# Seven-product MLP: where operand sums, stored parts, gate loads and down-step preparations stand in the program order

## The chip, the cores and the metric

The kernel runs on one core of a Trainium2 chip. The metric is the device time of one execution in microseconds (us); lower is better. A core has five engines that each work through their own list of instructions in order and wait for one another on semaphores: TensorE (PE, matrix products), VectorE (DVE), ScalarE (ACT), GpSimd (POOL) and SyncE (SP, which here only starts transfers). ACT and POOL can start transfers too; each of the three has a queue of its own, and the profile counts 16 DMA engines that carry them.

## The reference

Two transformer layers on 1024 tokens of width 1024. What bears on the change is the end of the first layer:

```
m  = g0 * y_a + g1 * y_b + g2 * y_c         # y_b = attn @ w_b
h  = h + m @ w_o
hn = rms_norm(h, norm2_g)
gate, up = split(hn @ w_gate_up)            # w_gate_up 1024 x 5632
h  = h + (silu(gate) * up) @ w_down         # w_down 2816 x 1024
mkv = rms_norm(mem) @ w_mem_kv              # second layer, prepared early
```

## The kernel before

Every float32 product is made of three passes: each operand is split into a high part (a rounded copy, made by ACT) and a low part (what is left, a subtraction, made by POOL or DVE, `lo_of`, L312). `mm3` (L283, L284, L285) issues high x high, high x low (or low x high) and low x high. A weight goes from a loaded tile `wraw` into two parts `wpart`: ACT L96 and POOL L97 for the plain stages, ACT L1233 and POOL L312 for the gate/up products.

The stages follow each other on PE in program order: **wb** (attention output times `w_b`), **mkv** (the memory projection, in two halves), **wo** (output projection, added to `h`), **mlp** (gate/up), **down**, and then the second layer. What each engine does is written out by hand, one call after the other; pools hand out the buffers, and an engine that is given an instruction whose input or buffer isn't ready waits, with all that stands behind it.

*wb.* 16 tiles of 128 x 512. Each needs a stored gate (`g1d`) and a stored partial sum (`mpart`), loaded one tile ahead by `load_gp` into two of four `ev` buffers. DVE L1079 multiplies the product with the gate, L1080 adds the partial sum, ACT L1081 makes the high part, POOL L312 the low part. Beside it run two side jobs that are advanced as PE work is issued: one that normalizes the memory rows `mrow` (ACT L316, DVE L1039) for PE to transpose (L1045), and one that builds a bias table `G` and writes it out (ACT L1027, `gd<-G`, 768 KB out of 4 partitions).

*wo.* Per token block t (8 of them, 128 tokens) and quarter j of the columns, `add_rows` adds the product to `h` (DVE L1140). `norm2_a` takes the sum of squares of both halves of a block's row (ACT L316) and stores it, `norm2_b` finishes the RMS norm (DVE, up to L329).

*mlp.* Gate/up and down are block products of 2 x 2 blocks made with seven products instead of eight (Winograd's form). The blocks of `hn` are (first or last four token blocks) x (first or second half of the columns). Each of the seven products p takes a sum of blocks as its moving operand, turned on PE (`turns`, L1146, into two `ax` buffers) and split by ACT L1149 and DVE L1150 into `tb` or `tm`. `T1` (POOL L1179) and `T3` (DVE L1180) are two of these sums, `sums24` (DVE L1497, POOL L1498) makes two more. The sums of the weights' blocks are `gu_sums` (DVE L1208 to L1210). One product (`gu_mm(n)`) is 12 matmuls of 512 columns; `gu_seq` is the order of the 154 products: unit 0 (gate) and unit 1 (up) of the first 256 columns are interleaved, all later units come one after the other. `gu_prep(n)` splits the weights of product n, `gu_out(n)` evacuates it. After each up unit, `hidden_sums` (POOL L1338 to L1341) makes the hidden blocks and sums that the down stage needs, and `store` writes them to DRAM (`hd`): three of the seven (`SPLIT`) as a high part (ACT L1303) and a low part (DVE L312). `at(n, f)` puts a store off to product n.

*down.* 77 steps (7 products x 11 pairs), four token blocks each, 12 matmuls of 512 columns a step. `dn_ahead(m)` loads step m+8, sums the weights of m+4 (L1450), makes high parts of m+3 (ACT L1466) and low parts of m+2 (DVE L312). `dn_open` does that for the first steps, ahead of the last two `gu_out`. The final norm of the first four blocks runs beside the last steps (DVE L329).

Of the kernel before, what the change touches and what calls it, by code (L numbers as in the profile page):

```python
# [117 lines left out]
def build(tc, A, out, dbg=None, stop=None):  # L118
# [1042 lines left out]
    ssq = {}  # L1161

    def norm2_a(t):

        ssq[t] = [work.tile([128, 4], F32, name="ss", bufs=4)[:, :1] for _ in range(2)]
        for c in range(2):
            sumsq(ht[t, c], ssq[t][c])
            nc.sync.dma_start(hres[t, :, 512 * c:512 * c + 512], ht[t, c])

    def norm2_b(t):  # L1170

        s0, s1 = ssq.pop(t)
        nc.vector.tensor_tensor(s0, s0, s1, op=ALU.add)
# [16 lines left out]
    gu_seq = [(0, 1), (0, 2), (1, 1), (1, 2)] + [(u, p) for p in (5, 7, 3, 4, 6) for u in (0, 1)]  # L1190
# [47 lines left out]
    for j in range(4):  # L1238
# [44 lines left out]
    acc, todo = {}, []  # L1283
# [14 lines left out]
    def store(p, pr, t):  # L1298
        if p not in SPLIT:
            nc.sync.dma_start(hd[p - 1, pr, :, :512], t)  # L1300
# [3 lines left out]
        lo_of(t.bitcast(F32R), t, hi, nc.vector)  # L1304
        nc.sync.dma_start(hd[p - 1, pr, :, :512], hi.bitcast(F32))
# [25 lines left out]
    def hidden_sums(u, n):  # L1331
# [84 lines left out]
    def dn_load(m):  # L1416
# [3 lines left out]
        p, i = dn_seq[m]  # L1420
        f1, f2 = (slice((2 * i + c) * 128, (2 * i + c) * 128 + 128) for c in (0, 1))
# [72 lines left out]
    def sums24(ts):

        for t in ts:
            nc.vector.tensor_tensor(ht[t + 4, 1], ht[t + 4, 1], ht[t, 0], op=ALU.subtract)  # L1497
            nc.gpsimd.tensor_tensor(ht[t, 1], ht[t, 1], ht[t + 4, 1], op=ALU.subtract)  # L1498
# [9 lines left out]
    gu_prep(5)  # L1508
    gu_mm(2, [(7, 0), (7, 1), (7, 2), (5, 3)])
    gu_out(2)  # L1510
    gu_mm(3, [(3, 3), (7, 3), (6, 0), (6, 1)])
    sums24((3,))
# [12 lines left out]
    for n in range(6, last - 1):
# [11 lines left out]
    run_todo(last + 9)  # L1537
    close(hbp)
    close(tbp)
# [3 lines left out]
    hpool = pool("h2", side="right")  # L1543
    h = hpool.tile([128, NT, D], F32, name="hh")
# [4 lines left out]
    hxp = pool("hx", side="right")  # L1549
    fg = hxp.tile([128, D], F32, name="fg")  # L1550
# [494 lines left out]
```

## Time and profile before

| what | value |
|---|---|
| time, median of 3 runs | 2262.42 us (2260.66 to 2262.77) |
| the profiled execution's own time | 2258.33 us |
| its span in the trace | 2256.6 us |
| busy: PE, DVE, POOL, ACT | 96%, 61%, 37%, 35% |
| mean granted TensorE clock | 0.986 of full |

The span is the time between the first and the last instruction that the trace shows; 1.73 us lie around it. Busy shares are means over the whole span. A matmul of 512 columns shows a duration of about 0.4 us, but the next one starts 0.23 us after it, since they are pipelined: distances between starts tell the pace. "PEclk" is the share of full speed that the clock throttle granted.

### The profile page before, as it was taken

Reading aid. Unit: us, or ns where it says so; the run is one execution under the profiler, and the core shown is the slowest. Engines: PE = TensorE matmul, PEld = TensorE weight load, DVE = VectorE, ACT = ScalarE, POOL = GpSimd, SP = SyncE. Lnnn points to the kernel's source line nnn. Section 1 sums busy time; section 2 is a strip of 40 time slices with the busy share of each in tenths; the row PEclk is TensorE's granted clock in tenths of the full one; section 3 lists DMA queues with packets and bytes.
Section 4 is the critical chain, followed back from the end, with each engine's and each line's share of the span. In section 5 each row is a group of like instructions: output and inputs, shape, how many; then the busy total and the mean of one; then the engine's idle time right before and its main releaser. Section 6 shows DMA issues by size and latency. Waiting matters only on the chain.

```text
span 2256.6 us, 31373 instructions
## 1 busy us (share of the span) xinstructions
PE 2166.0 (96%) x11855; PEld 1872.9 (83%) x11855; DVE 1382.1 (61%) x2712; ACT 785.9 (35%) x1548; POOL 840.0 (37%) x713
## 2 busy tenths in 40 slices
PE   7999999999999999989779999999999999999998
PEld 6789888998888888779767888888788799997998
DVE  6688899888883887321754545454675650922724
ACT  4573211211122876221232333333433342212631
POOL 0213322325542310852146878777100212661122
PEclk9999999999999999999889999999999999999999
DMA  4212122113320000444212433333998612120023
GB/s 146 70 66 73 57 77 76 48 47 103 109 88 19 20 1 10 161 120 158 80 42 84 145 108 128 125 112 106 322 341 320 207 57 80 38 66 19 1 70 137
DMA packets 150076, 227.84 MB, mean 101 GB/s; under 512 B 14896, under 2 KB 93972, under 8 KB 149924
## 3 DMA queue, kind: packets, MB, share of 16 engines
q1 hardware_dynamic: 131872, 179.85, 24.0%
q0 software_dynamic: 8096, 26.74, 3.2%
q10 hardware_dynamic: 9956, 19.24, 2.5%
q8 instruction: 93, 1.52, 0.3%
q14 instruction: 59, 0.48, 0.1%
HBM read 170.46 MB, written 55.31 MB: 100 GB/s over the span
## 4 chain that ended last, share of the span: by engine, by line
PE 84%; issue 4%; DVE 4%; DMA 3%; POOL 3%; ACT 2%; ACTq 0%; DVEq 0%; SPq 0%; POOLq 0%
PE mm L285 24%; PE mm L284 24%; PE mm L283 24%; PE ax L283 2%; PE ax L285 2%; PE ax L284 2%; PE mm L956 1%; PE ax L1928 1%; DMA ev<-mpart 1%; PE mm L1870 1%; POOL wpart L97 1%; PE mm L337 1%; DMA ev<-g1d 1%; DVE scores L565 1%; PE mm L1906 1%
## 5 line engine op out<-in xcount | busy, mean ns | idle before, releaser
L97 POOL TENSOR_TENSOR wpart<-wraw,wpart 128x1024 fp32r<-128x1024 f32 (+1 forms) x108 | 259.4, 2420 | 531.1 <-ACT wpart L96 510.9
L285 PE MATMUL mm<-xh,wpart 128*128 128x512 f32 (+2 forms) x736 | 269.9, 367 | 0.0
L284 PE MATMUL mm<-xl,wpart 128*128 128x512 f32 (+2 forms) x736 | 269.5, 366 | 0.0
L283 PE MATMUL mm<-xh,wpart 128*128 128x512 f32 (+2 forms) x736 | 269.0, 365 | 0.0
L608 DVE MAX8 m<-scores 128x8 f32<-128x272 f32 (+6 forms) x224 | 188.8, 843 | 6.4 <-POOL scores L570 0.2
L610 DVE MATCH_REPLACE8 scores<-m,scores 128x272 f32<-128x272 f32 (+6 forms) x224 | 185.0, 826 | 0.0
L283 PE MATMUL mm<-tm,wpart 128*128 128x512 f32 x440 | 175.2, 398 | 5.4 <-DVE ev L1392 5.4
L285 PE MATMUL mm<-tm,wpart 128*128 128x512 f32 x440 | 174.4, 396 | 0.0
L284 PE MATMUL mm<-tm,wpart 128*128 128x512 f32 x440 | 174.3, 396 | 0.0
L96 ACT ACTIVATE wpart<-wraw 128x1024 fp32r<-128x1024 f32 (+1 forms) x110 | 111.5, 1048 | 150.7 <-issue 80.5
L284 PEld LDWEIGHTS mm<-xl,wpart 128*128 128x128 f32 x736 | 138.5, 188 | 20.5
L283 PEld LDWEIGHTS mm<-xh,wpart 128*128 128x128 f32 x736 | 138.3, 188 | 20.3
L285 PEld LDWEIGHTS mm<-xh,wpart 128*128 128x128 f32 x736 | 138.3, 188 | 19.5
L283 PE MATMUL mm<-wpart,hh 128*128 128x256 f32 x512 | 142.6, 278 | 0.0
L284 PE MATMUL mm<-wpart,hh 128*128 128x256 f32 x512 | 142.2, 278 | 0.0
L285 PE MATMUL mm<-wpart,hl 128*128 128x256 f32 x512 | 142.1, 278 | 0.0
L312 POOL TENSOR_TENSOR wpart<-hb,wpart 128x512 fp32r<-128x512 f32 x88 | 119.0, 1360 | 36.0 <-ACT wpart L1233 36.0
L284 PE MATMUL mm<-wpart,tm 128*128 128x512 f32 x242 | 97.1, 401 | 9.8 <-DVE wpart L312 9.8
L283 PEld LDWEIGHTS mm<-tm,wpart 128*128 128x128 f32 x440 | 83.0, 189 | 25.2 <-DVE ev L1392 5.8
L285 PEld LDWEIGHTS mm<-tm,wpart 128*128 128x128 f32 x440 | 83.0, 189 | 20.0
L284 PEld LDWEIGHTS mm<-tm,wpart 128*128 128x128 f32 x440 | 83.1, 189 | 19.8
L312 POOL TENSOR_TENSOR wpart<-wraw,wpart 128x512 fp32r<-128x512 f32 x66 | 90.0, 1371 | 19.8 <-ACT wpart L1233 19.7
(385 smaller groups left out, 5747.8 us busy)
## 6 DMA issues: line engine op xcount, KB each, us to landing
wraw<-in_w_in_dram SPq DMA_DIRECT2D x68, 512.0 KB, 3.5
hd<-hb SPq DMA_DIRECT2D x110, 256.0 KB, 2.2
tm<-in_w_down_dram SPq DMA_DIRECT2D x99, 256.0 KB, 5.3
wraw<-in_w_gate_up_dram SPq DMA_DIRECT2D x44, 512.0 KB, 4.5
tm<-hd SPq DMA_DIRECT2D x33, 512.0 KB, 7.3
wraw<-hd SPq DMA_DIRECT2D x33, 256.0 KB, 5.4
mpart<-ev POOLq DMA_DIRECT2D x32, 256.0 KB, 2.3
ev<-mpart POOLq DMA_DIRECT2D x32, 256.0 KB, 4.1
```

The source lines that it names most:

```text
L96: nc.scalar.activation(hi[:, :nk * w], r, AF.Copy)
L97: (low or nc.gpsimd).tensor_tensor(lo[:, :nk * w], r, hi[:, :nk * w].bitcast(F32), op=ALU.subtract)
L283: nc.tensor.matmul(o, sh, mh, start=start, stop=False, skip_group_check=more)
L284: nc.tensor.matmul(o, sh, ml, start=False, stop=False, skip_group_check=more)
L285: nc.tensor.matmul(o, sl, mh, start=False, stop=stop, skip_group_check=more)
L312: (eng or nc.gpsimd).tensor_tensor(out_lo, src, hi.bitcast(F32), op=ALU.subtract)
L337: nc.tensor.transpose(tp[:, k * 128:k * 128 + P], r[:, kk * 128:(kk + 1) * 128], ident[:P, :P])
L565: nc.vector.scalar_tensor_tensor(s, r, c["wr"][:, h:h + 1], s, op0=ALU.mult, op1=ALU.add)
L608: nc.vector.max(m8, s)
L610: nc.vector.match_replace(out=s, in_to_replace=m8, in_values=s, imm_value=TAKEN)
L956: nc.tensor.transpose(tp[:P, h * 128:(h + 1) * 128], lgs[h][:, k0:k0 + P], ident)
L1870: nc.tensor.matmul(o[:, a, :w], qp[:, hd, i * 128:i * 128 + 128], keys, start=True, stop=True, skip_group_check=True)
```

## The change

* `load_gp`: the gate and partial-sum loads of wb are issued by ACT and no longer by POOL.
* wo and the start of mlp: `norm2_a` is taken per half; the first halves follow the second quarter of `add_rows`. `gu_sums(0)` moves from t = 4 to t = 1. `T1` and `T3` leave `norm2_b`; T1 for the first three blocks stays on POOL (`t1_sum`, L1178), the fourth goes to DVE; T3 is L1182. `gu_prep(0)` and `gu_prep(1)` stand ahead of the last sum of squares but one, `gu_prep(2)`, `gu_prep(3)` behind the last. The last `norm2_b` and its sums come behind `gu_mm(0)`.
* The order of the first 14 products: p = 5, 7 of both units before p = 3, 4, 6, and another spread of the turns over them. `sums24` is split up into `t2_sum` (DVE) and `t4_sum` (POOL), which is put later.
* The stores of the hidden parts begin at product n+3 instead of n+1.
* down: sums, high parts and low parts one step further ahead (m+5, m+4, m+3), `dn_open` makes four high and three low parts, the stores that are left are spread over the first steps, the tiles that need the hidden buffers' space are made at step 6, and the reloads of `h` go to every odd step from 7. `W.ahead()` (next stage's first weights) moves from the fourth-last step to the last.

```
-            nc.gpsimd.dma_start(g, g1d[f, :, t0:t0 + n])
-            nc.gpsimd.dma_start(p, mpart[f, :, t0:t0 + n])
+            nc.scalar.dma_start(g, g1d[f, :, t0:t0 + n])
+            nc.scalar.dma_start(p, mpart[f, :, t0:t0 + n])
...
-        if t >= 4:
-            a, b = ht[t - 4, 0], ht[t, 0]
-            nc.gpsimd.tensor_tensor(a, b, a, op=ALU.subtract)
-            nc.vector.tensor_tensor(b, ht[t, 1], b, op=ALU.subtract)
+    def t1_sum(t, eng):
+
+        eng.tensor_tensor(ht[t, 0], ht[t + 4, 0], ht[t, 0], op=ALU.subtract)
+
+    def t3_sum(t):
+
+        nc.vector.tensor_tensor(ht[t + 4, 0], ht[t + 4, 1], ht[t + 4, 0], op=ALU.subtract)
...
-    gu_seq = [(0, 1), (0, 2), (1, 1), (1, 2)] + [(u, p) for p in (5, 7, 3, 4, 6) for u in (0, 1)]
+    gu_seq = [(0, 1), (0, 2), (1, 1), (1, 2), (0, 5), (0, 7), (1, 5), (1, 7)]
+    gu_seq += [(u, p) for p in (3, 4, 6) for u in (0, 1)]
...
             for t in range(NT):
                 add_rows(mh, ml, wo[j], t, j)
+                if j == 1:
+                    norm2_a(t, 0)
...
         if t:
             norm2_b(t - 1)
+        if t == 1:
+            gu_sums(0)
         add_rows(mh, ml, wo[3], t, 3)
-        if t < 7:
-            norm2_a(t)
-        if 2 <= t < 6:
-            first_turns(t - 2)
-        if t == 4:
-            gu_sums(0)
         if t == 6:
             gu_prep(0)
             gu_prep(1)
             gu_load(1)
-        if t == 7:
-            gu_prep(2)
-    norm2_a(7)
+        norm2_a(t, 1)
+        if 2 <= t < 6:
+            first_turns(t - 2)
+        if t >= 6:
+            t3_sum(t - 6)
+        if t >= 5:
+            t1_sum(t - 5, nc.gpsimd)
+    gu_prep(2)
+    gu_prep(3)
...
-            at(n + 1 + k // 2, lambda p=p, t=t: store(p, pr, t))
+            at(n + 3 + k // 2, lambda p=p, t=t: store(p, pr, t))
...
-        dn_sum(m + 4)
-        dn_hi(m + 3)
-        dn_lo(m + 2)
+        dn_sum(m + 5)
+        dn_hi(m + 4)
+        dn_lo(m + 3)
...
+    gu_mm(0, [(5, 0), (5, 1), (5, 2)])
     norm2_b(7)
-    gu_prep(3)
+    t3_sum(2)
+    t1_sum(3, nc.vector)
+    t3_sum(3)
     gu_prep(4)
-    gu_mm(0, [(5, t) for t in range(3)])
     gu_out(0)
-    gu_mm(1, [(3, t) for t in range(3)])
-    sums24(range(3))
+    gu_mm(1, [(7, 0), (7, 1), (7, 2)])
+    gu_prep(5)
+    gu_mm(2, [(5, 3), (3, 0), (3, 1)])
+    gu_out(2)
+    gu_mm(3, [(7, 3), (3, 2)])
+    for t in range(3):
+        t2_sum(t)
     gu_sums(1)
...
     for n in (last - 1, last):
         gu_out(n)
-    run_todo(last + 9)
-    close(hbp)
-    close(tbp)
...
     for m, (p, i) in enumerate(dn_seq):
+        if m < 7:
+            run_todo(last + 1 + m)
+        if m == 6:
+            assert not todo
+            dn_rows()
         dn_ahead(m)
-        if i in (1, 3, 5, 7) and h_load:
+        if m > 6 and m % 2 and h_load:
...
-        if p == 3 and i == NPAIR - TAIL - 1:
+        if m == len(dn_seq) - 1:
             W.ahead()
```

Three places show how instructions move. The first is ACT in wb, around the write of the bias table (`gd<-G`); `L1063` and `L1064` are the two loads of one tile, `mth<-mm` the evacuation of the turned memory rows:

```order
+L1063 DMA ev<-g1d 128x512
+L1064 DMA ev<-mpart 128x512
 L1027 DMA gd<-G 512x1x384
 L316 ACTIVATE junk,ss<-mrow 128x1024
 L1081 ACTIVATE mh<-ev 128x512
+L1063 DMA ev<-g1d 128x512
+L1064 DMA ev<-mpart 128x512
 L1050 ACTIVATE mth<-mm,vcols 128x128 x4
 L1081 ACTIVATE mh<-ev 128x512
```

The loads now stand in ACT's list between the splits, and those of later tiles come behind the table's write in ACT's own queue.

The second is ACT at the end of wo and the start of mlp; `wpart<-wraw` is the high part of a gate/up weight, `junk,ss<-hb` a sum of squares, `tm<-ax` the evacuation of turned operands:

```order
 L1149 ACTIVATE tb<-ax 128x4x128 x2
-L316 ACTIVATE junk,ss<-hb 128x512 x2
-L1233 ACTIVATE wpart<-wraw 128x512 x3
-L316 ACTIVATE junk,ss<-hb 128x512 x2
-L1233 ACTIVATE wpart<-wraw 128x512
-L1233 ACTIVATE wpart<-hb 128x512
+L1236 ACTIVATE wpart<-wraw 128x512 x2
+L316 ACTIVATE junk,ssq<-hb 128x512 x2
+L1236 ACTIVATE wpart<-wraw 128x512 x2
 L1149 ACTIVATE tm<-ax 128x4x128 x3
```

The weights of the first two products are split ahead of the last two sums of squares, which wait for the last blocks of `h`; those of the next two stay behind them.

The third is DVE at the first stores of hidden parts, before:

```order
L1328 TENSOR_TENSOR ev<-mm,ev 128x512 x2
L1208 TENSOR_TENSOR hb<-wraw 128x512
L1209 TENSOR_TENSOR hb<-hb,wraw 128x512
L1210 TENSOR_TENSOR hb<-wraw 128x512
L312 TENSOR_TENSOR hb<-hb 128x512
L1381 TENSOR_TENSOR ev<-mm,ev 128x512
L312 TENSOR_TENSOR hb<-hb 128x512 x2
L1392 TENSOR_TENSOR ev<-mm,ev 128x512
```

and now:

```order
L1211 TENSOR_TENSOR hb<-wraw 128x512
L1212 TENSOR_TENSOR hb<-hb,wraw 128x512
L1213 TENSOR_TENSOR hb<-wraw 128x512
L1391 TENSOR_TENSOR ev<-mm,ev 128x512
L312 TENSOR_TENSOR hb<-hb 128x512
L1402 TENSOR_TENSOR ev<-mm,ev 128x512
L312 TENSOR_TENSOR hb<-hb 128x512
L1327 TENSOR_TENSOR hb<-mm,ev 128x512
L312 TENSOR_TENSOR hb<-hb 128x512
```

The evacuations of the next products (L1381, L1392 before; L1391, L1402, L1327 now) come first, and the three low parts of the stores between them one at a time.

## Rows read from the trace of the kernel before

**Rows 1.** The page: busy us (share of the span) xinstructions, and the chain that ended last.

```profile
PE 2166.0 (96%) x11855; PEld 1872.9 (83%) x11855; DVE 1382.1 (61%) x2712; ACT 785.9 (35%) x1548; POOL 840.0 (37%) x713
...
PE 84%; issue 4%; DVE 4%; DMA 3%; POOL 3%; ACT 2%; ACTq 0%; DVEq 0%; SPq 0%; POOLq 0%
```

**Rows 2.** Waits of PE: for whom, us in total, times, longest us.

```profile
PE ax L1146 <- DVE tm L1150: 18.6, 3, 10.3
...
PE mm L284 <- DVE wpart L312: 9.8, 3, 4.3
```

**Rows 3.** PE at mlp's start: start, duration, instruction [idle before <- releaser].

```profile
1114.62 0.80 PE L283 MATMUL mm<-tb,wpart 128*128 128x512 f32 x1 [6.32 <-ACT wpart L1233]
...
1130.75 1.09 PE L1146 MATMUL ax<-ident,hb 128*128 128x128 f32 x4 [10.27 <-DVE tm L1150]
...
1132.06 0.63 PE L284 MATMUL mm<-tb,wpart 128*128 128x512 f32 x1
1132.49 0.63 PE L285 MATMUL mm<-tb,wpart 128*128 128x512 f32 x1
...
1138.91 0.40 PE L284 MATMUL mm<-tb,wpart 128*128 128x512 f32 x1
1139.14 0.39 PE L285 MATMUL mm<-tb,wpart 128*128 128x512 f32 x1
...
1148.85 1.09 PE L1146 MATMUL ax<-ident,hb 128*128 128x128 f32 x4 [6.34 <-DVE tm L1150]
```

**Rows 4.** ACT, DVE and POOL at mlp's start, each in order of time.

```profile
1113.33 0.63 ACT L316 ACTIVATE junk<-hb 128x512 bf16<-128x512 f32 x1 [6.25 <-DVE hb L1140]
...
1113.96 1.13 ACT L1233 ACTIVATE wpart<-wraw 128x512 fp32r<-128x512 f32 x2
...
1128.27 1.73 DVE L1180 TENSOR_TENSOR hb<-hb 128x512 f32<-128x512 f32 x1 [1.15 <-POOL hb L1179]
...
1140.87 5.01 POOL L1498 TENSOR_TENSOR hb<-hb 128x512 f32<-128x512 f32 x3 [9.74 <-DVE hb L1497]
```

**Rows 5.** A window: us, busy (x instructions) of each engine, PEclk, DMA share, GB/s.

```profile
1130.00:1140.00 10.00, 8.56 (x34) 6.73 (x35) 3.77 (x7) 2.99 (x5) 1.14 (x1) 0.66 0.00 0
```

**Rows 6.** wb, first memory rows: POOL, DVE and PE in order of time.

```profile
922.82 5.23 POOL L97 TENSOR_TENSOR wpart<-wraw,wpart 128x1024 fp32r<-128x1024 f32 x2
927.97 0.60 POOL L1063 DMA_DIRECT2D ev<-g1d  x1
...
932.60 0.69 DVE L1079 TENSOR_TENSOR ev<-mm,ev 128x512 f32<-128x512 f32 x1 [6.83 <-DMA ev<-g1d]
...
937.81 1.11 PE L1045 MATMUL mm<-ident,mrow 128*128 128x128 f32 x4 [5.45 <-DVE mrow L1039]
```

**Rows 7.** wb, bias table and end: ACT's queue, DVE, ACT, PE.

```profile
954.92 0.76 ACTq L1027 DMA_DIRECT2D gd<-G  x1
...
975.41 0.69 DVE L1079 TENSOR_TENSOR ev<-mm,ev 128x512 f32<-128x512 f32 x1 [7.27 <-DMA ev<-g1d]
...
1003.17 1.99 ACT L96 ACTIVATE wpart<-wraw 128x1024 fp32r<-128x1024 f32 x2
...
1004.26 0.58 PE L283 MATMUL mm<-wpart,mth 128*128 128x256 f32 x1 [5.39 <-ACT wpart L96]
```

**Rows 8.** DVE and PE at the first stores of hidden parts.

```profile
1207.97 3.41 DVE L312 TENSOR_TENSOR hb<-hb 128x512 fp32r<-128x512 f32 x2 [1.95 <-POOL hb L1341]
...
1212.04 0.80 PE L283 MATMUL mm<-tm,wpart 128*128 128x512 f32 x1 [5.36 <-DVE ev L1392]
```

**Rows 9.** PE at the start of down.

```profile
1601.02 0.80 PE L284 MATMUL mm<-wpart,tm 128*128 128x512 f32 x1 [4.27 <-DVE wpart L312]
```

**Rows 10.** DVE and PE at the end of down.

```profile
1796.43 6.70 DVE L329 SCALAR_TENSOR_TENSOR hh<-hh,ry,pg 128x1024 f32<-128x1024 f32 x2
...
1803.78 0.80 PE L284 MATMUL mm<-wpart,tm 128*128 128x512 f32 x1 [4.18 <-DVE wpart L312]
```

**Rows 11.** The page's DMA issues: count, KB each, median us to landing.

```profile
hd<-hb SPq DMA_DIRECT2D x110, 256.0 KB, 2.2
```

More of the change, by code (lines that the diff above doesn't have):

```diff
@@ L1159, in build, with norm2_a @@
     TM = {}
[L1161 to L1168, printed above, removed]
+    ssq = work.tile([128, 2 * NT], F32, name="ssq")
+    def norm2_a(t, c):
+        sumsq(ht[t, c], ssq[:, 2 * t + c:2 * t + c + 1])
+        nc.sync.dma_start(hres[t, :, 512 * c:512 * c + 512], ht[t, c])
     def norm2_b(t):
-        s0, s1 = ssq.pop(t)
-        nc.vector.tensor_tensor(s0, s0, s1, op=ALU.add)
+        s0 = ssq[:, 2 * t:2 * t + 1]
+        nc.vector.tensor_tensor(s0, s0, ssq[:, 2 * t + 1:2 * t + 2], op=ALU.add)
         y = rstd_b(rstd_a(s0))
@@ L1299, in store @@
         if p not in SPLIT:
+            stored.setdefault(pr, set()).add(p)
             nc.sync.dma_start(hd[p - 1, pr, :, :512], t)
@@ L1304, in store @@
         lo_of(t.bitcast(F32R), t, hi, nc.vector)
+        assert p not in stored.setdefault(pr, set())
+        stored[pr].add(p)
         nc.sync.dma_start(hd[p - 1, pr, :, :512], hi.bitcast(F32))
@@ L1488, in dn_open, with t2_sum, t4_sum @@
             dn_load(m)
-        for m in range(3):
+        for m in range(4):
             dn_hi(m)
-            if m < 2:
+            if m < 3:
                 dn_lo(m)
[L1494 to L1498, printed above, removed]
+    def t2_sum(t):
+        nc.vector.tensor_tensor(ht[t + 4, 1], ht[t + 4, 1], ht[t, 0], op=ALU.subtract)
+    def t4_sum(t):
+        nc.gpsimd.tensor_tensor(ht[t, 1], ht[t, 1], ht[t + 4, 1], op=ALU.subtract)
+    gu_mm(0, [(5, 0), (5, 1), (5, 2)])
     norm2_b(7)
-    gu_prep(3)
+    t3_sum(2)
+    t1_sum(3, nc.vector)
+    t3_sum(3)
     gu_prep(4)
-    gu_mm(0, [(5, t) for t in range(3)])
     gu_out(0)
-    gu_mm(1, [(3, t) for t in range(3)])
-    sums24(range(3))
-    gu_sums(1)
[L1508 to L1512, printed above, removed]
+    gu_mm(1, [(7, 0), (7, 1), (7, 2)])
[5 more added lines that the diff above has]
+        t2_sum(t)
+    gu_sums(1)
+    gu_prep(6)
+    gu_mm(4, [(3, 3), (6, 0)])
+    t2_sum(3)
     gu_out(1)
     gu_out(3)
-    gu_prep(6)
+    gu_out(4)
     gu_prep(7)
-    gu_mm(4, [(6, 2), (4, 0), (4, 1), (4, 2)])
-    gu_out(4)
+    gu_mm(5, [(6, 1), (6, 2)])
+    gu_out(5)
+    for t in range(4):
+        t4_sum(t)
     gu_prep(8)
+    gu_mm(6, [(6, 3), (4, 0)])
+    gu_out(6)
     gu_prep(9)
-    gu_mm(5, [(6, 3), (4, 3)])
-    gu_out(5)
-    ahead = 10
+    gu_mm(7, [(4, 1), (4, 2)])
+    gu_out(7)
+    gu_prep(10)
+    gu_mm(8, [(4, 3)])
+    gu_out(8)
+    ahead = 11
     last = len(gu_seq) - 1
-    for n in range(6, last - 1):
+    for n in range(9, last - 1):
         while ahead <= min(n + 6, last):
@@ L1536, in build, with dn_rows @@
         gu_out(n)
[L1537 to L1539 removed]
     MARK("down")
[L1543 to L1544 removed]
     h_load = [(t, c) for ts, c in ((range(4, 8), 1), (range(4), 0), (range(4, 8), 0), (range(4), 1))
               for t in ts]
[L1549 to L1556 removed]
+    def dn_rows():
+        close(hbp)
+        close(tbp)
+        DN["hpool"] = pool("h2", side="right")
+        DN["h"] = DN["hpool"].tile([128, NT, D], F32, name="hh")
+        DN["hxp"] = pool("hx", side="right")
+        DN["fg"] = DN["hxp"].tile([128, D], F32, name="fg")
+        DN["pg2"] = DN["hxp"].tile([128, D], F32, name="pg2")
+        nc.gpsimd.dma_start(DN["fg"], A["final_g"].rearrange("(a d) -> a d", a=1).to_broadcast([128, D]))
+        nc.gpsimd.dma_start(DN["pg2"], A["pre_norm_g_2"].to_broadcast([128, D]))
+        DN["ttp"] = pool("tt", side="right")
+        DN["tt"] = DN["ttp"].tile([128, NPAIR, 512], F32, name="tt")
+        DN["du2"] = DN["ttp"].tile([128, 4, 512], F32, name="du2")
     def down_mm(o, m, t, start, stop, more):
@@ L1641, in build @@
     MARK("fin")
-    close(ttp)
+    close(DN["ttp"])
     close(tmp_)
+    h, hpool, hxp = DN["h"], DN["hpool"], DN["hxp"]
     yp = pool("y", side="left")
```

15 lines of the change are left out of this document (6 added, 9 removed).

## The prediction

> **What bounds the kernel now.** I read the page first. PE is busy for 2166.0 us, 96% of the span, and makes up 84% of the chain that ended last [rows 1]: the kernel is a row of matmuls with about 90 us of holes, and an edit that adds no PE work can give back only holes, and the slow clock that follows them. The second view is PE's waits [rows 2], the third the order of time around each of the long ones [rows 3 to 10]. Five places concern this change. (A) In wb, PE waits 5.45 us for the memory rows and 5.39 us for the last weights of mkv [rows 6, 7]. (B) At mlp's start it waits 6.32, 10.27 and 6.34 us [rows 3]. (C) At the first stores of hidden parts 5.36 us [rows 8]. (D) At the start of down 4.27 us [rows 9]. (E) At its end two waits that with D make the 9.8 us of [rows 2], so 5.5 us, 4.18 of it in one [rows 10].
>
> **Behind each hole the clock is low.** After the 10.27 us wait two neighbouring matmuls start 0.43 us apart (1132.06, 1132.49), and later 0.23 us (1138.91, 1139.14) [rows 3]; the window has a granted clock of 0.66 [rows 5], a mixture of the levels 1.2 and 2.4 GHz. So some 6 us are worked at half pace behind a long wait, and about 3 us are lost on top of it; behind waits of 4 to 5 us I estimate 1.5 to 3. Twelve matmuls at full pace, one gate/up product or one down step, are 12 x 0.23 = 2.8 us, and the 24 of a wb tile 5.6 us.
>
> **(A) Gate loads on ACT's queue.** In POOL's list the load issued at 927.97 stood behind two low parts of weights that took 5.23 us, and DVE got its gate at 932.60, so that DVE's norm of the memory rows came too late [rows 6]. On ACT the load stands behind two high parts instead (1.99 us for two, [rows 7]) and waits for POOL only until the buffer's last reader (L312) is through, which comes ahead of the low parts in POOL's list. I get the norm's end at about 932, where PE arrives at 937.81 - 5.45 = 932.36: hole and slow clock go, 5.45 + 3 = 8.5 us. What the edit adds: 32 issues in ACT's list (0.6 us each by POOL's row), each waiting there for its buffer; ACT's splits queue behind them, and DVE and PE behind those. A tile's chain (gate product, sum, high part, low part, issue, landing) is about 8 us for two tiles of 11.2 us of PE, so this is hidden as long as loads land in some 4 us.
>
> They do not, once the bias table is written: with the table issued at 954.92, the gate load issued just behind it let DVE go on only at 975.41, 20 us later [rows 7], though it had another queue. Behind the table, on ACT's own queue, I don't expect it sooner. PE runs ahead on its product buffers meanwhile and pays at the end, when ACT splits the last weights at 1003.17 [rows 7]. Bounds: the table is issued about 4 us earlier, since the gates before it come sooner; if the later gates land as long after their issue as now, their loads save up to 8 us more, because they no longer stand behind POOL's low parts: 12. If they wait for the end of the table, only the 4 remain. I take 8, between the two, since the row shows a long wait but not a full one.
>
> The Trainium skill (DMA: Bandwidth & Descriptors, "Issuing engines are not separate DMA queues") says that starting transfers from another engine saves only the sequencer's time for the issue. By that A would give the 1.2 us of one pair of issues, and the sum below would be 7 us smaller. The trace differs: what held the load at 927.97 was 5.23 us of other work in the issuing engine's list [rows 6], which the rule doesn't count.
>
> **(B) Start of mlp.** Now: the first product's weight parts stand on ACT behind a sum of squares that waits 6.25 us for DVE [rows 4], hence the 6.32; the turns wait for DVE's L1150, which stands behind the last block's norm and behind T3, which waits for POOL's T1 (1.15, then 1.73 us beside POOL) [rows 4], hence the 10.27; and three sums on DVE with three on POOL of 5.01 us [rows 4] stand ahead of the next L1150, hence the 6.34. With the third L1146 wait (18.6 - 10.27 - 6.34 = 2.0) and three slow stretches the loss is 6.3 + 18.6 + 9 = 34 us.
>
> After: the first two weights are split ahead of the last sums of squares, so PE goes on at 1108.3 without the 6.32. The third turn of operand 5 needs the first of two `ax` buffers back. Its evacuation on ACT stands behind the last sum of squares, which I put at 1114 to 1115 (a block later than the one at 1113.33, but without DVE's wait on POOL), and two weight parts (1.13, [rows 4]), then ACT and DVE at 0.6 to 0.7 each: 1117.4. PE is there at about 1112: a wait of 5.3, and 3 us of clock. The last norm comes behind gu_mm(0)'s turns now, and is needed only for turns of blocks 3 and 7 and for T1, T3; I estimate 1.6 us there and 2.5 in shorter waits. That leaves 12 of 34: a gain of 22. Bounds: 34 if none of it appears; 14 if the third turn and the norm wait 4 us longer each, for instance because T1 on POOL and T3 on DVE slow each other as 1.73 us shows.
>
> **(C) Stores.** DVE's two low parts (3.41 us) wait for POOL's last sum, and the evacuation behind them holds PE [rows 8]. Now the evacuation is ahead of them and the three low parts stand one by one between evacuations, two products (5.6 us) later, when POOL is through. The gain is 5.36 and some clock: 6 (5 to 7). In the ten steady pairs PE has no holes, so nothing is gained there.
>
> **(D) Start of down.** The low part that PE misses at 1601.02 [rows 9] stood behind three store parts; now three steps' low parts are ready before them. One step ahead is 2.8 us, the reordering gives the rest: 4.27 + 1.6 = 6; 0 if the loads, not the order, are what is late.
>
> **(E) End of down.** The low part behind two L329 of 6.70 us (slowed by POOL's L97) comes no earlier, but is needed one step of 2.8 us later: of 4.18 remain 1.4, and the clock stays up. 5.5 + 3.3 - 1.4 = 7.4; I take 6 (2 to 9), since `W.ahead` stands elsewhere and L97 with it.
>
> **Sum.** 8 + 22 + 6 + 6 + 6 = 48. Against the profiled execution: 2258.3 - 48 = 2210.3 (its span and 1.7 us around it shrink alike); it was 4.1 us under the median of the runs, so 2214 on the scale of the median. All upper bounds: 12 + 34 + 7 + 6 + 9 = 68, so 2194; all lower: 4 + 14 + 5 + 0 + 2 = 25, so 2237.
>
> **Rivals.** (1) *The gates wait for the whole table.* Then A is 4 and the time 2218. For it: 20 us for a load on another queue already looks like standing in line. Against: if queues share the DMA engines anyway, one queue need be no worse than two. The Trainium skill (the same page, "Queues, rings and completion order") says that an engine takes the descriptors of one ring in order, which is this case; no row of the trace shows two transfers so on one queue.
> (2) *mlp's waits only move.* If the third turn's wait is as long as the 10.27 now, because ACT does two more splits ahead of it, B is about 10 and the time 2226. For it: ACT, DVE and POOL have the same sums to do in the same 40 us, and PE's waits there all hang on that chain. Against: the 6.32 is undone by order alone.
> (3) *All of it goes*: 2194.
> (4) *Slower: the steady pairs start to wait.* Stores come two products later, and the buffers of the next up unit's blocks (19 `hb` in all) come free only when a store has landed, 2.2 us after its issue [rows 11]. A low part takes up to 1.7 us beside POOL (3.41 for two, [rows 8]); with 0.3 for the issue that is 4.2 us, against 2.8 us to the next evacuation, so DVE can be 1.4 us late, which PE's accumulators cover for a product. If they don't cover it, each of ten pairs pays. At 4.8 us per pair it eats the 48; at 6, with a slow clock each time, the time is 2274.
>
> **Numbers.** Chances: forecast 0.36; (1) 0.26; (2) 0.20; (3) 0.10; (4) 0.05; gains and waits that cancel within 4.5 us 0.03. Predicted 2214. The forecast, (1) and (2) with their own scatter of 8 us, and most of (3), lie between 2198 and 2240. 0.2% (4.5 us) is about what a measurement of this kernel can tell from no change: faster 0.92, same 0.03, slower 0.05.
>
> **What would show it.** PE has no wait for L1039 at the first memory rows; the wait for mkv's last weights is there still, after gates that land late; no wait of PE at the first gate/up weights, one of about 5 us at a turn shortly after, and two fewer windows at 0.66; none at C and D; about 1.4 us at E; full pace through the ten pairs. The prediction is wrong if PE waits inside the pairs, if loads fall behind at the start of down, or if ACT, held by a gate load, splits weights too late.

## The result and the profile after

| kernel | median of the runs (lowest to highest) | profiled execution | its span |
|---|---|---|---|
| before | 2261.54 us (2254.11 to 2262.77, 4 runs) | 2258.33 us | 2256.6 us |
| after | 2232.47 us (2231.19 to 2232.91, 4 runs) | 2231.19 us | 2229.5 us |

The ratio is 0.9877, with a 95% interval from 0.9855 to 0.9899: 29 us faster where 48 were forecast, which is 18 us over the forecast time and inside the range. The next table has, from both traces, where PE starts a stage's first matmul, and where the output projection's last one is through:

| PE reaches, us | before | after | gained in the stage ahead |
|---|---|---|---|
| gated projection (wb) | 891.71 | 892.15 | -0.4 |
| output projection (wo) | 1014.18 | 1016.96 | -2.3 |
| end of wo | 1108.30 | 1113.83 | -2.8 |
| down | 1590.85 | 1562.35 | +34.0 |
| last stage | 1821.64 | 1789.14 | +4.0 |
| last matmul | 2248.35 | 2221.02 | -5.2 |

These sum to 27.3, and the two profiled executions differ by 27.1. So nearly all of the gain is that of the MLP's stage. Down gains 4.0, and two stretches lost time: 5.5 us up to wo's end, and 5.2 in the last stage, which the change doesn't touch.

The page's first row (columns as in [rows 1]): PE has 66 us of holes left of 91.

```profile
PE 2163.4 (97%) x11855; PEld 1879.5 (84%) x11855; DVE 1379.5 (62%) x2713; ACT 785.9 (35%) x1548; POOL 817.6 (37%) x680
```

PE's waits after: for whom, us in total, times, longest us (before: [rows 2]).

```profile
PE ax L1146 <- DVE tm L1150: 7.6, 3, 6.1
PE mm L284 <- DVE wpart L312: 6.9, 4, 3.0
PE mm L283 <- ACT wpart L96: 5.7, 2, 4.8
PE mm L284 <- POOL wpart L97: 3.4, 2, 2.5
...
PE mm L285 <- POOL wpart L97: 2.7, 1, 2.7
```

The turns cost 7.6 us of waiting instead of 18.6. The waits for weights (L96, L97) are those at wb's end, 10.9 us in four pieces where before had the 5.39 of [rows 7] and 2.14. In order of time on PE, two new waits in wb and wo, then the places of [rows 3, 8, 9, 10]:

```profile
958.66 0.66 PE L1045 MATMUL mm<-ident,mrow 128*128 128x128 f32 x4 [3.24 <-DVE mrow L1039]
...
1071.50 0.39 PE L284 MATMUL mm<-wpart,mh 128*128 128x256 f32 x1 [0.98 <-POOL wpart L97]
...
1113.83 0.40 PE L283 MATMUL mm<-tb,wpart 128*128 128x512 f32 x1
...
1123.10 1.09 PE L1146 MATMUL ax<-ident,hb 128*128 128x128 f32 x4 [6.11 <-DVE tm L1150]
...
1193.18 0.50 PE L283 MATMUL mm<-tm,wpart 128*128 128x512 f32 x1 [1.23 <-DVE hb L1327]
...
1588.16 0.79 PE L284 MATMUL mm<-wpart,tm 128*128 128x512 f32 x1 [2.98 <-DVE wpart L312]
...
1774.15 0.50 PE L284 MATMUL mm<-wpart,tm 128*128 128x512 f32 x1 [2.12 <-DVE wpart L312]
```

The first gate/up product starts without a wait. The third turn of operand 5 waits 6.11 us, and ACT's list shows why: the turn buffer's evacuation (L1149) stands behind the last sum of squares and two weight parts, as forecast.

```profile
1119.98 0.63 ACT L316 ACTIVATE junk<-hb 128x512 bf16<-128x512 f32 x1 [4.40 <-DVE hb L1140]
...
1120.61 1.13 ACT L1236 ACTIVATE wpart<-wraw 128x512 fp32r<-128x512 f32 x2
1121.65 1.06 ACT L1149 ACTIVATE tm<-ax 128x512 fp32r<-128x512 f32 x2
```

Windows at the MLP's start and at the start of down (columns as in [rows 5]): one slow window behind the turn, and in down the DMA engines are full when PE waits.

```profile
1120.00:1130.00 10.00, 6.22 (x19) 4.64 (x20) 7.32 (x17) 5.02 (x10) 4.44 (x4) 0.52 0.07 26
1130.00:1140.00 10.00, 8.10 (x46) 6.28 (x44) 5.91 (x10) 4.11 (x7) 1.29 (x1) 0.97 0.01 2
...
1580.00:1590.00 10.00, 7.02 (x27) 4.76 (x25) 3.19 (x6) 1.75 (x4) 1.11 (x2) 0.90 0.99 335
```

The 10 us behind the wait in down, after and then before:

```profile
1588.00:1598.00 10.00, 9.84 (x28) 7.07 (x29) 7.93 (x14) 5.94 (x11) 0.35 (x1) 0.66 0.98 355
```

```profile
1601.00:1611.00 10.00, 9.98 (x36) 7.93 (x37) 7.80 (x13) 6.90 (x13) 1.11 (x2) 0.83 1.00 335
```

In down, DVE makes that low part only after a load has come:

```profile
1586.81 0.69 DVE L1461 TENSOR_TENSOR tt<-tm 128x512 f32<-128x512 f32 x1 [7.85 <-DMA wraw<-hd]
```

In wb, PE's wait at the first memory rows [rows 6] is gone, as forecast; at the second ones it waits 3.24 us, where before had 1.74. What the table then does (ACT's queue, DVE, PE; before: [rows 7]):

```profile
952.89 0.76 ACTq L1027 DMA_DIRECT2D gd<-G  x1
...
953.78 9.20 ACTq L1063 DMA_DIRECT2D ev<-g1d  x1
...
963.07 3.65 ACTq L1064 DMA_DIRECT2D ev<-mpart  x1
966.77 0.37 ACT L1050 ACTIVATE mth<-mm,vcols 128x128 fp32r<-128x128 f32 x1 [11.40 <-PE mm L284]
...
987.15 0.69 DVE L1079 TENSOR_TENSOR ev<-mm,ev 128x512 f32<-128x512 f32 x1 [8.62 <-DMA ev<-g1d]
...
1005.65 0.58 PE L283 MATMUL mm<-wpart,mth 128*128 128x256 f32 x1 [4.79 <-ACT wpart L96]
1008.70 0.58 PE L284 MATMUL mm<-wpart,mth 128*128 128x256 f32 x1 [2.47 <-POOL wpart L97]
```

The gate load issued behind the table took 9.20 us to issue alone, and ACT's own work stood behind it until 966.77. DVE got that gate at 987.15, 33 us after the issue began; in the run with the table on POOL's queue below, the table itself takes 34.7 us to land.

At the end of down, DVE and POOL:

```profile
1760.83 0.69 DVE L312 TENSOR_TENSOR wpart<-tm,wpart 128x512 fp32r<-128x512 f32 x1
...
1766.09 2.88 DVE L312 TENSOR_TENSOR wpart<-tm,wpart 128x512 fp32r<-128x512 f32 x1
1768.89 4.60 DVE L329 SCALAR_TENSOR_TENSOR hh<-hh,ry,pg 128x1024 f32<-128x1024 f32 x2
...
1765.58 5.64 POOL L97 TENSOR_TENSOR wpart<-wraw,wpart 128x1024 fp32r<-128x1024 f32 x2 [14.22 <-ACT wpart L96]
```

A low part of the same size takes 0.69 us alone and 2.88 while POOL subtracts. Three waits of 1.00, 2.12 and 0.84 us are left of the 5.5 there.

**A change of pace that nothing in the diff names.** After the first twenty-one, the gate/up products run without holes in both kernels, yet their matmuls start 0.2295 us apart where before has 0.2329. In the last stage, which is not edited, the 256-column ones start 0.1200 us apart where before has 0.1167. (Each is the mean distance between the starts of neighbouring matmuls of one shape, at full clock, distances over 0.262 or 0.135 us left out.) In the MLP's 1848 matmuls that is 6.3 us gained, in down's 924 (0.2290 to 0.2268) 2.0; in wo's 760 (0.1178 to 0.1200) 1.7 lost; in the last stage 2285 x 0.0033 = 7.5 lost and, with 309 wide ones (0.2328 to 0.2269), 1.8 gained. That makes 5.7 lost in the last stage, where the table has 5.2. By the profile the five nearly cancel (0.9 us gained), so the pace does not explain the 29 us; it explains the table's last line.

### The profile page after: what moved, and what is told of

The parts are those of the page before. It is cut to its first block, busy times and chain, and to the rows that moved or that the text cites. A ratio compares the mean times of both kernels' runs of the same rounds, so it can differ in the third digit from the quotient of the medians.

```text
span 2229.5 us, 31385 instructions
## 1 busy us (share of the span) xinstructions
PE 2163.4 (97%) x11855; PEld 1879.5 (84%) x11855; DVE 1379.5 (62%) x2713; ACT 785.9 (35%) x1548; POOL 817.6 (37%) x680
## 4 chain that ended last, share of the span: by engine, by line
PE 43%; DVE 3%; issue 2%; ACT 1%; POOL 1%; DMA 1%; SPq 0%; DVEq 0%; ACTq 0%; POOLq 0%
PE mm L283 13%; PE mm L284 13%; PE mm L285 13%; PE ax L1962 1%; PE mm L1904 1%; PE ax L284 1%; PE ax L283 1%; PE ax L285 1%; PE mm L1940 1%; PE mm L337 0%; DVE hb L329 0%; DVE wpart L312 0%; DMA wraw<-in_w_out_dram 0%; DVE tm L1150 0%; DVE hh L329 0%
## 5 line engine op out<-in xcount | busy, mean ns | idle before, releaser
L97 POOL TENSOR_TENSOR wpart<-wraw,wpart 128x1024 fp32r<-128x1024 f32 (+1 forms) x108 | 259.8, 2423 | 538.5 <-ACT wpart L96 536.7
L283 PE MATMUL mm<-tm,wpart 128*128 128x512 f32 x440 | 173.1, 393 | 1.2 <-DVE hb L1327 1.2
L285 PE MATMUL mm<-tm,wpart 128*128 128x512 f32 x440 | 171.7, 390 | 0.0
L284 PE MATMUL mm<-tm,wpart 128*128 128x512 f32 x440 | 171.2, 389 | 0.0
L96 ACT ACTIVATE wpart<-wraw 128x1024 fp32r<-128x1024 f32 (+1 forms) x110 | 111.5, 1048 | 134.6 <-issue 80.5
L283 PE MATMUL mm<-wpart,hh 128*128 128x256 f32 x512 | 145.2, 284 | 0.0
L284 PE MATMUL mm<-wpart,hh 128*128 128x256 f32 x512 | 144.9, 283 | 0.0
L283 PEld LDWEIGHTS mm<-tm,wpart 128*128 128x128 f32 x440 | 82.6, 188 | 18.8 <-DVE hb L1327 1.7
L283 PEld LDWEIGHTS mm<-wpart,hh 128*128 128x128 f32 x512 | 98.3, 192 | 0.1
L285 PEld LDWEIGHTS mm<-wpart,hl 128*128 128x128 f32 x512 | 98.3, 192 | 0.0
L284 PEld LDWEIGHTS mm<-wpart,hh 128*128 128x128 f32 x512 | 98.3, 192 | 0.0
```

Of the source, the lines that this page charges most:

```text
L96: nc.scalar.activation(hi[:, :nk * w], r, AF.Copy)
L97: (low or nc.gpsimd).tensor_tensor(lo[:, :nk * w], r, hi[:, :nk * w].bitcast(F32), op=ALU.subtract)
L283: nc.tensor.matmul(o, sh, mh, start=start, stop=False, skip_group_check=more)
L284: nc.tensor.matmul(o, sh, ml, start=False, stop=False, skip_group_check=more)
L285: nc.tensor.matmul(o, sl, mh, start=False, stop=stop, skip_group_check=more)
```

## The experiments

**Is the pace an accident of the execution?** The kernel before, unchanged.

> The kernel before, unchanged, once more with a profile, to tell what belongs to the kernel from what belongs to an execution. The changed kernel's trace shows other distances between matmuls: 0.230 us instead of 0.233 in gate/up, 0.120 instead of 0.118 in wo, 0.120 instead of 0.114 to 0.118 in the last stage. If these belong to the kernel, this run shows 0.233 in gate/up, 0.118 in wo and 0.114 in the last stage again, within 0.0005. If they belong to the execution or the chip, they differ from the first profile. Waits of PE as before: 6.3, 10.3 and 6.3 us at the start of mlp.

Measured: 2259.65 us (one run), with 0.2329 us in gate/up and 0.1178 in wo, as before. The last stage has 0.1173, where the first profile has 0.1167 by the same count (not the 0.114 that the expectation names). So the differences to the changed kernel belong to the program; the last stage's pace differs by 0.0006 between executions of one program.

**Gate loads back on POOL**, the rest of the change kept.

```diff
-            nc.scalar.dma_start(g, g1d[f, :, t0:t0 + n])
-            nc.scalar.dma_start(p, mpart[f, :, t0:t0 + n])
+            nc.gpsimd.dma_start(g, g1d[f, :, t0:t0 + n])
+            nc.gpsimd.dma_start(p, mpart[f, :, t0:t0 + n])
```

> The changed kernel with the gate loads back on POOL. Theory 1 (the loads stand behind the bias table's write on ACT's own queue, 33 us to landing, and the whole edit loses): wo ends about 5.5 us earlier than in the changed kernel (at 1108 instead of 1113.8), the first memory rows cost 5.4 us again and the last weights of mkv about 5.4; time about 2227. Theory 2 (forecast: the edit gains about 8 and what is late in wo comes from elsewhere, such as the slower matmuls): time about 2240.

Measured: 2228.89 us, ratio to before 0.9858 (0.9842 to 0.9875). The memory rows' first wait is back (3.99 us), and still the MLP starts at 1110.74 instead of 1113.83: edit A as a whole lost some 3 us.

**Gate loads on ACT alone**, in the kernel before (the diff above, reversed).

> The kernel before with nothing but the gate loads moved to ACT. Theory 1: slower by about 5.5 us (wo ends at about 1113.8), 2267 against 2261.5; PE waits 3 us or so for the second memory rows and about 5 and 2.5 for mkv's last weights. Theory 2 (the forecast's term): faster by 8, 2254.

Measured: 2264.24 us, ratio 1.0006 (0.9997 to 1.0016). The first issue behind the table takes 7.88 us, and wo starts at 1016.08 us, against 1012.99 in the unchanged kernel profiled beside it. A alone is worth nothing, or a small loss.

**The table on POOL's queue**, gates on ACT: does ACT's queue hold them, or the table?

```diff
-        nc.scalar.dma_start(gd, G.unsqueeze(1).to_broadcast([4, 128, 384]))
+        nc.gpsimd.dma_start(gd, G.unsqueeze(1).to_broadcast([4, 128, 384]))
```

> The changed kernel with the bias table written from POOL's queue instead of ACT's; the gate loads stay on ACT's queue. Theory 1 (order within one queue): no gate load takes more than about 6 us, no long issue on ACT (9.2 us now), PE does not wait for mkv's last weights (4.8 and 2.5 now), time about 2232 - 13 = 2219. Rival (the table keeps a few DMA engines busy, whichever queue it is on, and every load that needs them waits): gates behind it still take 10 to 20 us as in the kernel before, the last split is near 1000, time about 2226.

Measured: 2225.66 us, ratio 0.9841 (0.9826 to 0.9855). No issue takes 9 us any more, but DVE still waits 6.03 us for a partial sum and 6.07 us for a gate, loaded on another queue than the table's. The page's line for the table, with its landing time:

```profile
gd<-G POOLq DMA_DIRECT2D x1, 768.0 KB, 34.7
```

Part of A's loss was the queue; the rest of these waits follows the table into the other queue.

**The table behind the gated projection.**

```diff
-        yield 8.0
+        yield 1e6
         nc.scalar.dma_start(gd, G.unsqueeze(1).to_broadcast([4, 128, 384]))
```

> The kernel after with the bias table's write to memory issued after the last tile of the gated projection, not in its middle. Theory (the table, in whatever queue, keeps the gate loads from landing): no gate load takes over 6 us, the 3.2 us wait at the memory rows' second transposes and the four waits at its end (0.96, 2.71, 4.79, 2.47) go but for 2 or 3 us, the clock stays up there, the MLP starts at about 1102 instead of 1113.8: 2217 to 2222. Rival 1 (the gate loads wait for ACT's own work): the waits stay, 2231. Rival 2 (the table's write collides with what follows it, the weights of the output projection or the memory freed behind the memory rows): the waits move into the memory keys or the output projection, 2228 to 2236.

Measured: 2237.06 us, ratio 0.9887 (0.9870 to 0.9903). The gate loads are quick and wo starts at 1000.42, 16.5 us sooner, and then its own weights are late, so that the MLP starts at 1118.55. ACT waits for them 16.49 us:

```profile
1016.58 1.06 ACT L96 ACTIVATE wpart<-wraw 128x1024 fp32r<-128x1024 f32 x1 [16.49 <-DMA wraw<-in_w_o_dram]
```

Rival 2 holds: the table costs the next transfer.

**The table in the output projection**, its tile kept in `mpool`.

```diff
-    G = memp.tile([4, 384], F32, name="G")
+    G = mpool.tile([4, 384], F32, name="G")
...
         if t == 1:
             gu_sums(0)
+            nc.gpsimd.dma_start(gd, G.unsqueeze(1).to_broadcast([4, 128, 384]))
```

> The kernel after with the bias table kept in the pool of the scaled attention and written to memory in the output projection, by POOL at row tile 1 (about 1080), where the DMA engines are 0.07 to 0.28 busy. Theory (the table costs wherever other loads are due, and nothing here): the gate loads land within 5 us, no wait at the end of the gated projection, the memory keys' and the output projection's weights are there, the MLP starts at 1097 to 1102 instead of 1113.8: 2216 to 2221. Rival 1 (it then delays the first gate/up weights, due at 1105 to 1115): the MLP's start gives 5 or more back, 2222 to 2228. Rival 2 (weights of the memory keys or of the output projection are late of themselves, without the table): the waits there stay, over 2225.

Measured: 2236.05 us, ratio 0.9887 (0.9873 to 0.9902); both my theory and its rivals fell. POOL, ahead of PE, issued it at 1056, and the late transfer was one that I hadn't thought of: a store (`hres`), whose tile DVE's in-place norm must not overwrite before it has landed. PE stood 12.4 us behind it. DVE's row, then a window (columns as before) in which no engine works and little but the table moves:

```profile
1081.32 0.75 DVE L329 SCALAR_TENSOR_TENSOR hb<-hb,ry,ev 128x512 f32<-128x512 f32 x1 [17.48 <-DMA hres<-hb]
```

```profile
1070.00:1080.00 10.00, 0.00 (x0) 0.00 (x0) 0.00 (x0) 0.00 (x0) 0.00 (x0) 0.59 0.25 30
```

The DMA share is 0.25 for a transfer from 4 partitions, and it landed 34.5 us after its issue. The DMA packets in the trace show the late store itself: issued at 1058.22, it has moved 96 of its 128 packets by 1060.5, and the other 32, a quarter, go between 1072.4 and 1079.9, while never more than four of the table's packets are under way at once. So a transfer spread over all 16 engines has a quarter that waits on the four busy ones. The Trainium skill (DMA: Bandwidth & Descriptors, "Why a DMA increments its semaphore by 16 and not by 1") says that a transfer uses the largest number of engines up to 16 that divides the slowest dimension of both of its sides; for 4 partitions that is 4, and the 0.25 agrees.

**Stores of the last pair on POOL** (start of down).

```diff
+        q = nc.gpsimd if pr == NPAIR - 1 and p not in (1, 2) else nc.sync
...
-        nc.sync.dma_start(hd[p - 1, pr, :, 512:], t)
+        q.dma_start(hd[p - 1, pr, :, 512:], t)
```

> The kernel after with the stores of the last pair's parts (all but the first two) issued by POOL instead of SP. Theory (at the start of the down projection SP stands at a store, 1568.2 to 1574.2, and its loads behind it come late): the loads are issued some 5 us earlier, the 2.98 us wait at 1588 and the lower clock behind it (0.90, 0.76) go, 2227 to 2229. Rival (the loads are late because the DMA engines are full, 0.99 of them busy at 1575 to 1588): the wait stays within 1 us, 2231 to 2233. Third: POOL stands at these stores and its next work comes late, slower than 2234.

Measured: 2232.52 us, ratio 0.9864 (0.9849 to 0.9879). SP's loads for the twelfth step and on were issued from 1571.3 instead of 1576.0, and PE still waits 3.38 us, because DVE waits for a load:

```profile
1589.52 0.69 DVE L1462 TENSOR_TENSOR tt<-tm 128x512 f32<-128x512 f32 x1 [8.25 <-DMA tm<-in_w_down_dram]
...
1590.87 0.80 PE L284 MATMUL mm<-wpart,tm 128*128 128x512 f32 x1 [3.38 <-DVE wpart L312]
```

```profile
1580.00:1590.00 10.00, 7.49 (x34) 5.85 (x32) 1.75 (x4) 0.00 (x0) 0.58 (x2) 1.00 1.04 410
```

The rival holds: at the start of down the loads came no sooner for being issued sooner, with the DMA engines full; this order of the issues is not what makes them late.

**The third turn later; the last split later.**

```diff
-    gu_mm(0, [(5, 0), (5, 1), (5, 2)])
+    gu_mm(0, [(5, 0), (5, 1)])
...
-    gu_mm(1, [(7, 0), (7, 1), (7, 2)])
+    gu_mm(1, [(5, 2), (7, 0), (7, 1)])
...
-        if m == len(dn_seq) - 1:
-            W.ahead()
...
+    W.ahead()
     fa = Side(final_steps(range(4)))
```

> The kernel after with two edits that lie in different stages and are read apart by the stages' starts. First, the third turn of operand 5 goes from the first gate/up product to the second. Theory (PE waits there for a turn buffer that DVE and ACT empty late, behind the last norm): the six matmuls put ahead of it use up 1.4 to 2.4 us of the 6.1 us wait at 1123 and the rest stays, since the norm's work on DVE is the same. Rival (the wait is only that turn's own): it goes whole, the down projection starts 6 us sooner. Second, the split of the next weights (ACT and POOL) is emitted behind the last product of the down projection instead of ahead of it. Theory (DVE's lows and norms there are slow since POOL subtracts at the same time): the three waits of 4.0 us together fall under 1.5 and the clock of 0.83 there rises, 3 to 4 us. Rival (DVE simply has too much to do there): the waits stay within 1 us. Both theories: 2226 to 2228; both rivals' second parts and the first theory: 2230.

Measured: 2230.32 us, ratio 0.9865 (0.9850 to 0.9880). The MLP's stage took 446.9 us instead of 448.5, the 1.6 us of the theory; the wait is as long as ever, now at a product:

```profile
1124.53 0.80 PE L283 MATMUL mm<-tb,wpart 128*128 128x512 f32 x1 [6.08 <-ACT ev L1379]
```

So it is ACT's and DVE's work up to there that PE waits for, not one turn. The second edit moved nothing: POOL's subtraction ran at 1764.73, again beside DVE's low parts, and the three waits there are 3.9 us together as before. Whether POOL's part is what keeps E's waits is therefore untested.

**Addresses: before, shifted by 64 bytes.** In the compiled program the tiles that are laid out behind `ssq`, a new tile of the change, lie 64 bytes per partition further on: `mh`, `ml` (the scaled attention), `tm` and the last stage's `Y`, `hh` and `hl` among them. `tb`, `hb` and the weights' tiles stay where they were, so not every tile moves, though the expectation says so.

```diff
     ssq = {}
+    shift = work.tile([128, 16], F32, name="shift")
+    nc.gpsimd.memset(shift, 0.0)
```

> The kernel before with one unused 64-byte tile in the pool of small work tiles, so that every tile from the scaled attention on lies 64 bytes per partition further on, as in the kernel after; nothing else differs but one small memset. Theory (the addresses set the pace of the matmuls): the mean distance of two 512-column matmuls in gate/up falls from 0.2329 to about 0.2295 us, and that of 256-column ones rises to about 0.120 us in the memory keys (from 0.1136) and in the last stage (from 0.117); the MLP stage is shorter by about 6 us, the last stage longer by 5 to 7, the time within 3 us of before, 2259 to 2264. Rival (the pace comes from the order of the instructions or the waits between them): all three distances stay, 2262.

**Addresses: after, shifted by 192 bytes more.**

```diff
-    ssq = work.tile([128, 2 * NT], F32, name="ssq")
+    ssq = work.tile([128, 64], F32, name="ssq")
```

> The kernel after with its tile of squared sums widened from 64 to 256 bytes per partition, so that the tiles behind it lie where they lay before plus 256 bytes. Theory (addresses set the pace, by their remainder): the distances of before come back (0.233 us in gate/up, 0.1136 in the memory keys, 0.117 in the last stage); MLP stage from 448.5 to about 455 us, the part from the output projection's start to the MLP and the last stage shorter by about 7 together; time 2231 to 2235. Rival (order of instructions): the distances stay at 0.2295, 0.120 and 0.120, 2232. A mixture would say that the remainder is to a larger number than 256.

Measured: 2257.88 us, ratio 0.9982 (0.9972 to 0.9992), and 2235.10 us, ratio 0.9883 (0.9866 to 0.9899). Each took over the other kernel's pace, but for the last stage of the second, which comes near it. Windows of the shifted before, then of the padded after; 100 us of gate/up hold 438 matmuls in the first and 431 in the second (before 431, after 438), 50 us of the last stage 420 and 427 (before 439, after 419):

```profile
1300.00:1400.00 100.00, 100.00 (x438) 81.61 (x437) 52.23 (x56) 32.93 (x58) 76.68 (x55) 1.00 0.34 114
...
1900.00:1950.00 50.00, 50.00 (x420) 50.00 (x419) 30.48 (x104) 14.39 (x30) 24.42 (x25) 1.00 0.20 53
```

```profile
1300.00:1400.00 100.00, 100.00 (x431) 80.68 (x430) 49.41 (x57) 34.68 (x61) 74.53 (x54) 1.00 0.39 132
...
1900.00:1950.00 50.00, 50.00 (x427) 50.00 (x426) 46.04 (x156) 14.49 (x33) 33.58 (x43) 1.00 0.09 23
```

In distances: 0.2296, 0.1199 (wo) and 0.1200 us (last stage) in the first; 0.2329, 0.1178 and 0.1181 in the second. So the pace moves with the addresses. Gate/up holds a control of its own: from before to before shifted, the matmuls whose moving operand lies in `tm`, which moved, went from 0.2330 to 0.2281 us, and those with `tb`, which did not, from 0.2326 to 0.2335. By its trace the shift alone gains 0.6 us (2257.68 against 2258.33), by the medians 4.

**Each stage its own remainder.**

```diff
     mpool = pool("m", side="left")
+    nc.gpsimd.memset(mpool.tile([128, 16], F32, name="shift1"), 0.0)
...
     yp = pool("y", side="left")
+    nc.gpsimd.memset(yp.tile([128, 16], F32, name="shift2"), 0.0)
```

> The kernel after with one unused 64-byte tile ahead of the scaled attention's tiles and one ahead of the last stage's, so that these stages have the addresses' remainder of before (a multiple of 128 bytes) and the MLP and down projection keep that of after. Theory (each stage's pace follows its own tiles' remainder): 256-column matmuls at 0.1136 us in the memory keys, 0.1178 in the output projection and 0.117 to 0.118 in the last stage, 512-column ones at 0.2295 in gate/up and 0.2268 in down, 0.233 in the last stage: 2 us less up to the MLP, 4 to 5 less after the down projection: 2225 to 2228. Rival (the pace hangs on something else that the two earlier runs moved along): the last stage stays at 0.120 or gate/up goes back to 0.233, 2231 or more.

Measured: 2221.26 us, ratio 0.9822 (0.9805 to 0.9838), better than the theory, which doesn't explain the surplus: it had 0.1178 and 0.117 to 0.118. Gate/up keeps 0.2295 us; wo has 0.1141 and the last stage 0.1146 and 0.2289, faster than in either kernel. The last stage is 8.7 us shorter than in after.

**The table from all partitions, with the gains found.** The two pads, the third turn in the second product, and:

```diff
-    G = memp.tile([4, 384], F32, name="G")
+    G = memp.tile([128, 384], F32, name="G")
...
-        nc.scalar.dma_start(gd, G.unsqueeze(1).to_broadcast([4, 128, 384]))
+        nc.scalar.dma_start(gd.rearrange("h (p r) c -> (h p) r c", r=4),
+                            G.unsqueeze(1).to_broadcast([128, 4, 384]))
```

> The kernel after with three edits, read apart by the stages' starts: the two 64-byte tiles of the run called pads (2221.3); the third turn of operand 5 in the second product, as in the run called b_e; and a bias table built on 128 partitions, 32 for each head, and written from all of them in place of 4, the same 768 KB at the same place in ACT's order. Theory (the table costs since it leaves from 4 partitions and keeps a quarter of the DMA engines busy for some 30 us, so that every transfer over all 16 waits for those): it lands in under 8 us, the gate loads in under 6, the waits at the end of the gated projection and the memory keys fall from 13 to under 3 us, the output projection starts at 1000 to 1003 instead of 1017.8 and, with no transfer left to hold it, the MLP at 1093 to 1097 instead of 1110.6; 2202 to 2208. Rival 1 (768 KB cost what they cost, however spread): the waits stay above 8 us, 2213 to 2220. Rival 2 (the output projection's own loads, x and weights, then come late, as the stage starts sooner): the MLP starts at 1100 to 1106, 2209 to 2216.

Measured: 2207.49 us, ratio 0.9764 (0.9750 to 0.9778), faster than both kernels. The table lands in 5.4 us. The page's line, and PE's waits from 890 to 1140 (columns as above):

```profile
gd<-G ACTq DMA_DIRECT2D x1, 768.0 KB, 5.4
```

```profile
PE mm L283 <- ACT ev L1385: 7.3, 2, 6.1
PE mm L1051 <- DVE mrow L1045: 3.9, 2, 3.1
PE mm L284 <- POOL wpart L97: 2.2, 3, 1.1
```

Of the waits for weights 1.1 us are left at mkv and 1.1 in wo (the last line); the second memory rows still cost 3.1. Wo starts at 1002.75 (1017.76 with the pads alone) and the MLP at 1097.57 (1110.61). A transfer in the same queue, at the same place and of the same size no longer keeps DVE waiting for a gate or a partial sum once all partitions send it.

## Why the prediction held, and where it failed

**(A) failed, in its lower bound.** The step was "If they wait for the end of the table, only the 4 remain". They did wait for it, and A then lost about 3 us instead of gaining 8 (3.1 at the MLP's start, against the run with the loads back on POOL); alone it gave a ratio of 1.0006. Of the 5.5 us lost up to wo's end 2 are pace and 1 is the new wait in wo. The first half of the step came near: behind the first memory rows PE is 7.6 us ahead of before, against 8.5. It then loses 3.1 at the second memory rows (whose 1.74 us of before stood in no term of the sum), 5.9 where mkv begins and 0.9 up to wo. Rival 1 had the mechanism and the wrong price. Two things were not counted: an issue behind the table in the same queue holds the engine itself (9.20 us of ACT), and the argument "one queue need be no worse than two" looked at queues where the engines under them were the bound. With the table spread, PE reaches the MLP at 1097.57 where before ended wo at 1108.30: 10.7 us, of which half a us is pace (0.1171 us in wo). That is the moved loads and the spread table together; no run has the spread table with the loads on POOL, so what A alone is worth then stays open.

**(B) and (C) held.** From wo's end to down 34.0 us went, 6.3 of them pace; 27.7 are left against 22 + 6. The two can be told apart: counted from wo's end and without the pace, PE is 22.3 us ahead at the fifteenth gate/up product, 27.9 at the twenty-first and 27.7 at the last. The wait at the third turn is 6.11 against 5.3, behind the very instructions named; at the stores 1.23 us are left of 5.36. The run with the turn moved shows that the rest is ACT's and DVE's backlog. Rival 2 asked for 10.27 us there.

**(D) and (E) were mis-sized.** Together 1.9 us (4.0 less 2.1 of pace) instead of 12. D gained nothing: at the eleventh step PE is 0.5 us behind before, leaving out the pace: the wait fell from 4.27 to 2.98, but the granted clock in the 10 us behind it is 0.66 instead of 0.83. That is its lower bound, "0 if the loads, not the order, are what is late": with earlier issues the wait stayed, the DMA engines being full. E gained 2.4, near its lower bound of 2. Its step "of 4.18 remain 1.4" failed: 3.96 us are left in three waits. DVE is busy without a gap from 1762.50 to the last low part at 1775.22, so a step of lead is used up there. POOL's part in the slow rows fits the Trainium skill (SBUF — State Buffer, "SBUF: two separate sides": DVE and GpSimd share a pair of ports, one of them has it for a whole instruction, and the other stands); the rows of 0.69 and 2.88 us agree, but no run here took the overlap away.

**(4) and (3) were not it.** PE has no wait within the ten steady pairs; and D and E left too much for all to go.

**What no step held:** the pace, shown to move with the addresses. It shifted time between stages and hid itself in the sum.

**What was luck.** A came out 7 us under its lower bound, and D and E lay close to theirs. The time is in the range all the same because the range adds up all five lower bounds, and B and C, at 27.7 us, lay 9 above theirs.

## What to carry to other kernels

Before moving a load to another queue, ask which DMA engines the transfer ahead of it occupies: one that leaves from 4 partitions holds a quarter of them for as long as it takes, and every wide transfer in any queue waits for those; write it from all partitions instead. Follow stores, too, to whoever may not overwrite their source. And compare stages that the change doesn't touch: a new small tile can shift the tiles that are laid out behind it.

## What was not expected of the hardware

| kernel | address of `mh`, of `hh` | gate/up 512 | wo 256 | last stage 256 | last stage 512 |
|---|---|---|---|---|---|
| before | 75136, 107904 | 0.2329 | 0.1178 | 0.1167 | 0.2328 |
| after, and before shifted | 75200, 107968 | 0.2295 | 0.1200 | 0.1200 | 0.2269 |
| after padded | 75392, 108160 | 0.2329 | 0.1178 | 0.1181 | 0.2330 |
| after with two pads | 75264, 108032 | 0.2295 | 0.1141 | 0.1146 | 0.2289 |

Addresses are bytes in a partition, in the compiled program; gate/up's operands lie in `tm` and `tb`, `tm` at 75136, 75200, 75392 and 75200, `tb` at 196576 and on in all. With little but the addresses changed (one or two unused tiles, or a wider one), matmuls of one shape at full clock start 1.5 to 5% closer or further apart, and what is good for one stage is bad for another.

The addresses are not all of it. In wo the pads' kernel and the last one read the very same addresses, and yet the first 576 matmuls start 0.1133 to 0.1135 us apart in the one and 0.1178 in the other; near the stage's end the first slows to 0.1167 and the second quickens to 0.1145. The means 0.1167 and 0.1173 of before's last stage, in two executions of one program, are mixtures of these two paces as well. What chooses between them, which remainder is best, and why, stays open.
